# Band and cross probabilities in one tile, with 2 KB rows in the transfers inside SBUF

## The chip, the cores and the metric

The kernel runs on one core of a Trainium2 chip. The time is the device time of one execution in microseconds; below it is the median of three runs. A profile of one further execution gives the trace that the prediction reads. TensorE is PE (and PEld for its weight loads), VectorE is DVE, ScalarE is ACT, GpSimd is POOL, and SP is the engine that issues most of the DMA transfers.

## The reference

One layer of a decoder trunk is computed for a prompt of 4096 tokens and for 8 sequences of 8 new tokens ("sample"). The model width is 1024. What the kernel computes for the prompt, cut to the core:

```python
h = rmsnorm(x, g_pre);  z = h @ w_in                      # one combined projection
out_a = silu(cg) * cb * conv3(cc * ch)                    # 256 channels
o_b = window attention, 8 heads of 64 in 2 kv groups,     # 128-query blocks, keys of this
      window 128, one learned sink per head               # and the previous block
out_b = silu(ag) * o_b
o_c = cross attention, 4 heads of 64, into 256 memory tokens
out_c = silu(mg) * o_c
y = concat(out_a, out_b, out_c) @ w_out
result = x + rmsnorm(y, g_post)
```

For the sample the same layer runs with cached window keys and values, cached memory keys and values and a cached convolution state.

## The kernel before

The kernel has two stages. The first, up to about 970 us, is the input projection: TensorE multiplies split fp32 operands (a high and a low part) in a seven-product scheme. Near its end the first two groups of attention (`early_scores`, `early_transposes`, `early_values`) are put between its products.

The second stage runs over 33 blocks of 128 tokens (block 32, the sample, goes before block 31). `Block.run` multiplies the gated mix of one block with `w_out`: two halves of 512 columns, each of 8 x 3 matmuls (high by high, low by high, high by low) into one PSUM bank, `y_0` and `y_1`. Between these matmuls it runs the events of `events_of(i)`, keyed by the half and the step at which they come. Block i works on three attention groups at once:

- `values_and_scores(i)` at (0, 0): `Group.scores` multiplies queries and keys of group i + 3 (PSUM tiles `ws`, band, and `xs`, cross), then `Group.values` multiplies the finished probabilities of group i + 1 with the values (PSUM tile `pv`) and multiplies the result into the gates (`mix` or `place`); then the softmax of group i + 3 ends.
- `turn(0, i + 3)` and `turn(1, i + 3)` at (1, 2): `turn_band` and `turn_cross` transpose the probabilities on VectorE in 32 x 32 squares, and transfers inside SBUF move the squares to their partitions.
- `turn(2, i + 2)` at (0, 4): `masks` applies the window's two triangles on GpSimd to the moved band probabilities.
- `blocks[i + 1].split` at (1, 3): the next block's mix is split in a high part (ACT) and a low part (DVE) for TensorE.

Band probabilities of a group are in a tile `sm`, cross probabilities in a tile `xp`, each of 128 x 1024 fp32. Odd groups have a buffer of their own in the pool `wp`; even groups take theirs from the pool `work`, which has three buffers of 4 KB per partition. `moved` issues 16 transfers for one tile, 32 partitions by 1 KB each, so that a group takes 32 of them on SP:

```python
src = squares.rearrange("p (k n) -> p k n", k=4)
for g in range(4):
    for k in range(4):
        DMA.dma_start(to[32 * k : 32 * k + 32, g], src[32 * g : 32 * g + 32, k])
```

The end of a block is in two tails that run in the next block's `scores`: `scale` (the root mean square; the power is taken on GpSimd) and `store` (VectorE multiplies by that factor and adds the residual `xr`, line 1581; SP stores the result to `o_yp`). `xr` has two buffers, so that the load for block b + 2 on SP waits until the store of block b has landed. The other transfers on SP in this stage are `vh` (values of a group) and, for every second block, the gates of a chunk of 256 tokens (`mix` or `place`, 1 MB). Keys and queries of a chunk (`kst`, `q`) are loaded by GpSimd's queue.

Instructions are placed by a scheduler, except those that `keep_in_program_order` pins on their engine: in the blocks 1 to 30 all of VectorE's (`InOrder`), the masks, the high part of the split, and the attention's matmuls after the first (`tiled`). In the order that comes out, `y_0` of a block (18 or all 24 of its matmuls) stands between the scores and the values.

Of the kernel before, what the change touches and what calls it, by code (L numbers as in the profile page):

```python
# [8 lines left out]
F32 = mybir.dt.float32  # L9
# [3 lines left out]
ALU = mybir.AluOpType  # L13
AX = mybir.AxisListType

P = 128
D = 1024
KT = D // P
# [33 lines left out]
def hybrid_layer(ctx: ExitStack, tc: tile.TileContext, a: dict):  # L52
    nc = tc.nc
    TE, S, G, DMA = nc.tensor, nc.scalar, nc.gpsimd, nc.sync
# [981 lines left out]
    def work(name):  # L1036

        return third["work"].tile([P, D], F32, tag="u", name=name)

    run_open = [False]  # L1040

    def tiled(o, w, x, **kw):
# [69 lines left out]
    class Group:  # L1112
# [6 lines left out]
        def open_scores(self, n):  # L1119
            b = self.b  # L1120
            if n == 0:
                t = wp.tile([P, D], F32, tag="sm", name=f"sm{b}", bufs=1) if b % 2 and b > 1 else work(f"sm{b}")
                self.sm = t.rearrange("p (h k j) -> p h k j" if b < 2 else "p (k h j) -> p h k j", h=8, k=4)
                self.flat_sm = t
            if n == 3:
                t = wp.tile([P, D], F32, tag="p", name=f"xp{b}", bufs=1) if b % 2 and b > 1 else work(f"xp{b}")
                self.p = t.rearrange("p (h a k j) -> p h a k j" if b < 2 else "p (k h a j) -> p h a k j", h=4, a=2, k=4)
                self.flat_p = t

        def early_scores(self, n):  # L1130
            self.open_scores(n)
# [12 lines left out]
        def scores(self):  # L1144
            self.open_scores(0)
            self.open_scores(3)
# [50 lines left out]
        def band_weights(self):  # L1197
            n, (es, den, rd) = 8, self.band_sums
            V.tensor_tensor(den, den, es, op=ALU.add)
            V.reciprocal(rd, den)  # L1200
            V.tensor_scalar(rd, rd, 0.5, None, op0=ALU.mult)
            flat = self.flat_sm.rearrange("p (h k) -> p h k", h=n) if self.b < 2 else self.flat_sm.rearrange("p (k h j) -> p k h j", h=n, k=4)
# [19 lines left out]
        def early_transposes(self, n):  # L1222
            if n == 0:
                pt = work(f"wpt{self.b}").rearrange("p (u n) -> p u n", u=2)
                pv = work(f"wpv{self.b}").rearrange("p (u n) -> p u n", u=2) if self.b else None
                for u in range(2):
                    self.pt[u], self.pv[u] = pt[:, u], pv[:, u] if self.b else None
            if n == 2:
                xpt = work(f"xpt{self.b}").rearrange("p (u n) -> p u n", u=2)
                for u in range(2):  # L1230
                    self.xpt[u] = xpt[:, u]
            if n < 2:
                self.band_transposes(n, psum(0, f"wt{self.b}_{n}"))
            else:
                self.cross_transposes(n - 2, psum(0, f"xt{self.b}_{n}"))

        def moved(self, squares, name):

            tc.keep_in_program_order(V.transpose(squares, squares))
            to = wp.tile([P, 4, 256], F32, tag=name, name=f"{name}{self.b}")  # L1240
            src = squares.rearrange("p (k n) -> p k n", k=4)
            for g in range(4):
                for k in range(4):
                    DMA.dma_start(to[32 * k : 32 * k + 32, g], src[32 * g : 32 * g + 32, k])
            return to

        def turn_band(self):
            self.w = self.moved(self.flat_sm, "wt").rearrange("p g (h i) -> p g h i", h=8)

        def turn_cross(self):  # L1250
            self.x = self.moved(self.flat_p, "xt").rearrange("p g (h a i) -> p g h a i", h=4, a=2)

        def masks(self):

# [176 lines left out]
    def sample_window():  # L1431
# [22 lines left out]
        both = work("ssm")[:, : 4 * 192].rearrange("p (a n) -> p a n", a=4)  # L1454
# [30 lines left out]
        pt, ptn = work("swpt").rearrange("p (a n) -> p a n", a=2)[:, 0], work("swptn")[:64, :512]  # L1485
# [21 lines left out]
    class Block:  # L1507
# [28 lines left out]
        def run(self, last, events):  # L1536
# [6 lines left out]
            for p, (c0, c1) in enumerate(parts):  # L1543
                if b == 0:
                    both = values_psum("y0") if p == 0 else both
                    acc = both[:, p]
                else:
                    acc = (values_psum(f"y{b}_1")[:, 1] if p == 1 else psum(p // 2, f"y{b}_{p}"))[:, : c1 - c0]
                j, passes = 0, 3 if m == P else 2
                for k in range(KT):  # L1550
                    for fn in events.get((min(p, 1), k), ()) if p < 2 else ():
                        fn()
                    for l, r in ((0, 0), (1, 0), (0, 1)) if m == P else ((0, 0), (0, 1)):
                        TE.matmul(acc, self.hl[l][:, k], wo[k][c0 // 512][:, r, c0 % 512 : c0 % 512 + c1 - c0], start=j == 0, stop=j == passes * KT - 1)  # L1554
                        j += 1
                if m < P:
                    S.copy(yn[:m, c0:c1], acc[m : 2 * m])
                    V.tensor_tensor(acc[:m], acc[:m], yn[:m, c0:c1], op=ALU.add)
                end = last and p == 2
                if not end:  # L1560
                    V.tensor_tensor(yn[:m, c0:c1], acc[:m], gpost[:m, c0:c1], op=ALU.mult)
                square = lambda acc=acc, p=p, c0=c0, c1=c1, end=end: S.activation(  # L1562
                    (psum(2, "sq") if end else acc)[:m, : c1 - c0], acc[:m], AF.Square, scale=float(D) ** -0.5, accum_out=st[:m, p : p + 1])
                if p == 0 or last or b == 32:
                    square()
                if last and p == 1:
                    V.tensor_tensor(st[:m, 0:1], st[:m, 0:1], st[:m, 1:2], op=ALU.add)
# [9 lines left out]
                    V.tensor_tensor(yn[:m, 768:D], acc[:m], gpost[:m, 768:D], op=ALU.mult)  # L1577

            def store():
                for cs in (slice(0, 512), slice(512, D)) if last else (slice(0, D),):  # L1580
                    V.scalar_tensor_tensor(self.xr[:m, cs], yn[:m, cs], st[:m, 3:4], self.xr[:m, cs], op0=ALU.mult, op1=ALU.add)  # L1581
                    DMA.dma_start(dst[:, cs], self.xr[:m, cs])
# [23 lines left out]
    def events_of(i):  # L1606
# [3 lines left out]
        def at(p, k, fn, *args):  # L1610
            ev.setdefault((p, k), []).append(lambda: fn(*args))
# [141 lines left out]
```

## Time and profile before

| | |
|---|---|
| median of three runs | 1812.81 us (1812.52 to 1813.56) |
| the profiled execution | 1814.48 us, span 1812.8 us |
| mean granted clock of TensorE in it | 0.926 |
| PE busy | 1537.6 us (85%) |
| PEld busy | 1380.1 us (76%) |
| DVE busy | 1197.3 us (66%) |
| ACT busy | 732.0 us (40%) |
| POOL busy | 344.2 us (19%) |
| SP's DMA queue (q1) | 194501 packets, 262.47 MB, 46.9% of 16 engines |
| POOL's DMA queue (q0) | 40800 packets, 69.76 MB, 14.8% |

A row of the timeline has the start, the duration, the engine, the line of the kernel, the operation, what it writes and reads, and how many instructions are merged in the row; a bracket gives the idle time before it and what ended that. SPq is SP issuing transfers. A row of the waits has who waited for whom, the time in total, the number of waits and the longest. A row of the groups has the instructions of one line and form, their number, busy time, mean duration in ns, and the idle time before them.

### The profile page before, as it was taken

The numbers are of one execution on the slowest core, as the hardware profiler recorded it, in microseconds if no ns is written. First come the engines' busy times: TensorE is split into PE (matmuls) and PEld (weight loads), VectorE is DVE, ScalarE is ACT, GpSimd is POOL, SyncE is SP. The second block draws the span as 40 slices with busy tenths as digits, with TensorE's granted clock in tenths as the row PEclk, the third lists the DMA queues.
The fourth block names the chain that finished last, engine by engine and source line by source line (L and its number), as shares of the span: only waits on it lengthen the run. The fifth ranks groups of instructions, "written<-read, shape, count | busy, mean of one in ns | idle before, by whom it ended". The sixth has DMA issues, their size and how long they took to land. (4 is left out here: it accounts for less than half of the span.)

```text
span 1812.8 us, 31491 instructions
## 1 busy us (share of the span) xinstructions
PE 1537.6 (85%) x11471; PEld 1380.1 (76%) x11471; DVE 1197.3 (66%) x1920; ACT 732.0 (40%) x1844; POOL 344.2 (19%) x522
## 2 busy tenths in 40 slices
PE   9999999999999999999995776678667766777548
PEld 9999999999999999999994555456555555555336
DVE  7788888998877797677684654455546545654414
ACT  6766565642222244454362333333333333333212
POOL 0223332230000000001002322233123223322200
PEclk9999999999999999999997898888888888988679
DMA  9989998776432379677877455543554554343342
GB/s 259 215 230 268 269 237 297 245 211 233 165 107 107 121 258 306 222 238 231 247 286 204 131 158 156 154 113 121 150 156 133 155 156 138 111 136 116 121 157 82
DMA packets 236175, 335.29 MB, mean 185 GB/s; under 512 B 62453, under 2 KB 164853, under 8 KB 235989
## 3 DMA queue, kind: packets, MB, share of 16 engines
q1 hardware_dynamic: 194501, 262.47, 46.9%
q0 software_dynamic: 40800, 69.76, 14.8%
q8 instruction: 91, 1.49, 0.4%
q10 hardware_dynamic: 720, 1.05, 0.2%
q14 instruction: 63, 0.52, 0.1%
HBM read 192.54 MB, written 110.15 MB: 167 GB/s over the span
## 5 line engine op out<-in xcount | busy, mean ns | idle before, releaser
L1554 PE MATMUL y<-wo,mh 128*128 128x512 f32 (+1 forms) x1040 | 340.2, 400 | 41.3 <-DVE sm L62 13.1
L1554 PEld LDWEIGHTS y<-wo,mh 128*128 128x128 f32 x1040 | 198.4, 192 | 103.1 <-issue 33.5
L377 DVE TENSOR_TENSOR z<-c,z 128x520 f32<-128x520 f32 (+1 forms) x308 | 195.0, 646 | 88.8 <-PE c L370 88.0
L1554 PE MATMUL y<-wo,ml 128*128 128x512 f32 (+1 forms) x520 | 204.8, 394 | 0.0
L1044 PE MATMUL pv<-xt,mv 128*64 128x128 f32 x480 | 54.4, 398 | 176.6 <-DMA xt<-xp 108.8
L1044 PEld LDWEIGHTS pv<-xt,mv 128*64 128x64 f32 x480 | 43.9, 207 | 188.2 <-issue 181.8
L1212 ACT ACTIVATE xp<-xs,xnm 128x256 f32<-128x256 f32 x128 | 58.9, 473 | 260.8 <-issue 127.7
L1220 POOL TENSOR_SCALAR xp<-xp,xrd 128x256 f32<-128x256 f32 x128 | 62.4, 502 | 490.5 <-DVE xrd L62 404.0
L1195 ACT ACTIVATE sm<-sm,wnm 128x128 f32<-128x128 f32 x256 | 99.1, 389 | 116.9 <-DVE wnm L62 113.8
L62 DVE TENSOR_TENSOR mix<-mix,pv 128x256 f32<-128x256 f32 (+1 forms) x32 | 16.3, 551 | 159.0 <-PE pv L1044 153.8
L1554 PEld LDWEIGHTS y<-wo,ml 128*128 128x128 f32 x520 | 100.2, 193 | 20.5 <-issue 2.0
L62 DVE TENSOR_TENSOR place<-place,pv 128x256 f32<-128x256 f32 (+1 forms) x28 | 14.3, 551 | 134.3 <-PE pv L1044 134.3
L1178 ACT COPY sm<-ws 128x256 f32<-128x256 f32 x128 | 41.2, 376 | 68.1 <-PE ws L1044 43.2
L1562 ACT ACTIVATE y<-y 128x512 f32<-128x512 f32 (+1 forms) x66 | 38.4, 582 | 72.4 <-DVE yn L62 63.8
L1258 POOL TENSOR_SCALAR_AFFINE_SELECT wd<-wt 128x512 f32<-128x512 f32 (+1 forms) x60 | 60.8, 1013 | 32.0 <-DMA wt<-sm 16.5
L1044 PEld LDWEIGHTS ws<-kst,q 64*128 64x128 f32 x768 | 48.9, 190 | 11.6 <-issue 5.6
L62 DVE SCALAR_TENSOR_TENSOR xr<-yn,yst,xr 128x1024 f32<-128x1024 f32 x30 | 42.8, 1427 | 21.1 <-POOL yst L1575 21.0
L1044 PE MATMUL ws<-kst,q 64*128 64x256 f32 x768 | 56.5, 293 | 0.0
L1044 PE MATMUL pv<-wt,vh 128*64 128x256 f32 x240 | 53.0, 583 | 0.0
L745 POOL MEMSET negs<- 128x1 f32 x1 | 0.1, 98 | 264.4 <-PE c L370 264.4
L283 ACT ACTIVATE nat<-nat 104x1024 f32<-104x1024 f32 x40 | 42.2, 1056 | 15.7 <-DMA nat<-in_x_p 15.7
L1195 ACT ACTIVATION_READ_ACCUMULATOR sm<-sm,wnm 128x1 f32 x256 | 48.1, 188 | 0.0
(979 smaller groups left out, 4971.0 us busy)
## 6 DMA issues: line engine op xcount, KB each, us to landing
q<-qd POOLq DMA_DIRECT2D x32, 768.0 KB, 9.1
xr<-in_x_p SPq DMA_DIRECT2D x32, 512.0 KB
nat<-in_x_p SPq DMA_DIRECT2D x39, 416.0 KB
o_yp<-xr SPq DMA_DIRECT2D x31, 512.0 KB
wt<-sm SPq DMA_DIRECT2D x480, 32.0 KB
xt<-xp SPq DMA_DIRECT2D x480, 32.0 KB
md<-th POOLq DMA_DIRECT2D x48, 260.0 KB, 7.4
qd<-zh SPq DMA_DIRECT2D x48, 260.0 KB
```

Of the source, the lines that this page charges most:

```text
L62: return (lambda *args, **kw: tc.keep_in_program_order(fn(*args, **kw))) if self.on else fn
L283: S.activation(t[:RG], t[:RG], AF.Square, accum_out=r[:RG, i : i + 1])
L377: add = lambda dst, other: V.tensor_tensor(dst, c, other, op=ALU.add)
L745: G.memset(third["negs"], NEG)
L1044: ins = TE.matmul(o, w, x, **kw)
L1178: S.copy(to, squares(s3[:, :, P : 2 * P]))
L1195: S.activation(sm[:, h], sm[:, h], AF.Exp, bias=nm[:, h : h + 1], scale=SCALE, accum_out=den[:, h : h + 1])
L1212: S.activation(p[:, i], s[:, i].rearrange("p (a k j) -> p a k j", a=2, k=4), AF.Exp, bias=nm[:, i : i + 1], scale=SCALE, accum_out=den[:, ...
L1220: G.tensor_scalar(p[:, i], p[:, i], rd[:, i : i + 1], 0.5, op0=ALU.mult, op1=ALU.mult)
L1258: G.affine_select(out, src, pattern=[[32 * sign, 2], [0, 8], [sign, 32]], compare_op=op, fill=0.0, base=base * sign, channel_multiplier=-s ...
L1554: TE.matmul(acc, self.hl[l][:, k], wo[k][c0 // 512][:, r, c0 % 512 : c0 % 512 + c1 - c0], start=j == 0, stop=j == passes * KT - 1)
L1562: square = lambda acc=acc, p=p, c0=c0, c1=c1, end=end: S.activation((psum(2, "sq") if end else acc)[:m, : c1 - c0], acc[:m], AF.Square, sc ...
```

## The change

- One tile of 128 x 2048 holds band and cross probabilities. For group 2 and after, each of the four 32-column squares has 256 band columns and 256 cross columns side by side, so that one transfer moves 32 partitions by 2 KB: 16 transfers a group instead of 32. Even groups take the tile from `work` (now one buffer of each size), odd ones from `wp`. The two transposes stay separate; all transfers are issued after the second.
- The masks of group i + 2 move from event (0, 4) to (1, 1).
- The residual: ScalarE multiplies by the factor, and GpSimd adds `xr`, both pinned; VectorE's instruction goes, except for the last two blocks.
- The first matmul of each half-block, and the first after each event, are pinned. In the order that comes out, the values come right after the scores in every block, and all of `y_0` and `y_1` after them.
- The first groups and the sample's window reuse parts of the larger tile; the load of the sample's mask (`smraw`) comes earlier on SP.

```diff
-        third["work"] = right.enter_context(tc.tile_pool(name="work", bufs=3, side="right"))
+        third["work"] = right.enter_context(tc.tile_pool(name="work", bufs=1, side="right"))
...
+    def pair(name):
+
+        return third["work"].tile([P, 2 * D], F32, tag="uu", name=name)
...
+        def open_scores(self):
             b = self.b
+            t = wp.tile([P, 2 * D], F32, tag="s", name=f"s{b}", bufs=1) if b % 2 and b > 1 else pair(f"s{b}")
+            if b < 2:
+                self.flat_sm, self.flat_p = t[:, :D], t[:, D:]
...
+            else:
+                self.squares = t.rearrange("p (k n) -> p k n", k=4)
+                self.sm = self.squares[:, :, :256].rearrange("p k (h j) -> p h k j", h=8)
+                self.p = self.squares[:, :, 256:].rearrange("p k (h a j) -> p h a k j", h=4, a=2)
...
-        def moved(self, squares, name):
-
-            tc.keep_in_program_order(V.transpose(squares, squares))
-            to = wp.tile([P, 4, 256], F32, tag=name, name=f"{name}{self.b}")
-            src = squares.rearrange("p (k n) -> p k n", k=4)
+        def turn_band(self):
+            part = self.squares[:, :, :256]
+            tc.keep_in_program_order(V.transpose(part, part))
+
+        def turn_cross(self):
+            part = self.squares[:, :, 256:]
+            tc.keep_in_program_order(V.transpose(part, part))
+            to = wp.tile([P, 4, 512], F32, tag="w", name=f"w{self.b}")
             for g in range(4):
                 for k in range(4):
-                    DMA.dma_start(to[32 * k : 32 * k + 32, g], src[32 * g : 32 * g + 32, k])
-            return to
+                    DMA.dma_start(to[32 * k : 32 * k + 32, g], self.squares[32 * g : 32 * g + 32, k])
...
+                    ordered = b > 0 and (j == 0 or p < 2 and (min(p, 1), k) in events)
                     for l, r in ((0, 0), (1, 0), (0, 1)) if m == P else ((0, 0), (0, 1)):
-                        TE.matmul(acc, self.hl[l][:, k], ...)
+                        ins = TE.matmul(acc, self.hl[l][:, k], ...)
+                        if ordered:
+                            tc.keep_in_program_order(ins)
+                        ordered = False
...
             def store():
+                if not last and b != 32:
+                    tc.keep_in_program_order(S.mul(yn, yn, st[:, 3:4]))
+                    G.tensor_tensor(self.xr, yn, self.xr, op=ALU.add)
+                    DMA.dma_start(dst, self.xr)
+                    return
...
-        at(0, 4, turn, 2, i + 2)
+        at(1, 1, turn, 2, i + 2)
```

More of the change, by code (lines that the diff above doesn't have):

```diff
@@ L1038, in work, with in_order_here @@
         return third["work"].tile([P, D], F32, tag="u", name=name)
+    def pair(name):
+        return third["work"].tile([P, 2 * D], F32, tag="uu", name=name)
+    def in_order_here(ins):
+        if ps is not None:
+            tc.keep_in_program_order(ins)
     run_open = [False]
@@ L1117, in __init__, with early_scores @@
             self.pt, self.pv, self.xpt, self.cross_sums = {}, {}, {}, {}
-        def open_scores(self, n):
+        def open_scores(self):
             b = self.b
-            if n == 0:
[L1122 to L1131, printed above, removed]
+            t = wp.tile([P, 2 * D], F32, tag="s", name=f"s{b}", bufs=1) if b % 2 and b > 1 else pair(f"s{b}")
+            if b < 2:
+                self.flat_sm, self.flat_p = t[:, :D], t[:, D:]
+                self.sm = self.flat_sm.rearrange("p (h k j) -> p h k j", h=8, k=4)
+                self.p = self.flat_p.rearrange("p (h a k j) -> p h a k j", h=4, a=2, k=4)
+            else:
+                self.squares = t.rearrange("p (k n) -> p k n", k=4)
+                self.sm = self.squares[:, :, :256].rearrange("p k (h j) -> p h k j", h=8)
+                self.p = self.squares[:, :, 256:].rearrange("p k (h a j) -> p h a k j", h=4, a=2)
+        def early_scores(self, n):
+            if n == 0:
+                self.open_scores()
             if n < 2:
@@ L1144, in scores @@
         def scores(self):
-            self.open_scores(0)
-            self.open_scores(3)
+            self.open_scores()
             bands = [psum(n, f"ws{self.b}_{n}").rearrange("p (h k) -> p h k", h=2) for n in range(4)]
@@ L1201, in band_weights @@
             V.tensor_scalar(rd, rd, 0.5, None, op0=ALU.mult)
-            flat = self.flat_sm.rearrange("p (h k) -> p h k", h=n) if self.b < 2 else self.flat_sm.rearrange("p (k h j) -> p k h j", h=n, k=4)
+            flat = self.flat_sm.rearrange("p (h k) -> p h k", h=n) if self.b < 2 else self.squares[:, :, :256].rearrange("p k (h j) -> p k h j", h=n)
             rd = rd.unsqueeze(2).to_broadcast([P, n, P]) if self.b < 2 else rd.unsqueeze(1).unsqueeze(3).to_broadcast([P, 4, n, 32])
@@ L1224, in early_transposes @@
                 pt = work(f"wpt{self.b}").rearrange("p (u n) -> p u n", u=2)
-                pv = work(f"wpv{self.b}").rearrange("p (u n) -> p u n", u=2) if self.b else None
+                pv = self.flat_sm.rearrange("p (u n) -> p u n", u=2) if self.b else None
                 for u in range(2):
@@ L1235, in early_transposes @@
                 self.cross_transposes(n - 2, psum(0, f"xt{self.b}_{n}"))
-        def moved(self, squares, name):
-            tc.keep_in_program_order(V.transpose(squares, squares))
-            to = wp.tile([P, 4, 256], F32, tag=name, name=f"{name}{self.b}")
-            src = squares.rearrange("p (k n) -> p k n", k=4)
+        def turn_band(self):
[5 more added lines that the diff above has]
+            to = wp.tile([P, 4, 512], F32, tag="w", name=f"w{self.b}")
             for g in range(4):
                 for k in range(4):
-                    DMA.dma_start(to[32 * k : 32 * k + 32, g], src[32 * g : 32 * g + 32, k])
-            return to
[L1247 to L1251, printed above, removed]
+                    DMA.dma_start(to[32 * k : 32 * k + 32, g], self.squares[32 * g : 32 * g + 32, k])
+            self.w = to[:, :, :256].rearrange("p g (h i) -> p g h i", h=8)
+            self.x = to[:, :, 256:].rearrange("p g (h a i) -> p g h a i", h=4, a=2)
         def masks(self):
@@ L1453, in sample_window @@
         transpose_to(svn, [(zs[:, 5, :], 64)], 1, "svnt")
-        both = work("ssm")[:, : 4 * 192].rearrange("p (a n) -> p a n", a=4)
+        ssm = pair("ssm")
+        both = ssm[:, : 4 * 192].rearrange("p (a n) -> p a n", a=4)
         sms = [both[:, 2 * half : 2 * half + 2] for half in range(2)]
@@ L1484, in sample_window @@
         yield
-        pt, ptn = work("swpt").rearrange("p (a n) -> p a n", a=2)[:, 0], work("swptn")[:64, :512]
+        pt, ptn = ssm[:, D : D + 512], ssm[:64, D + 512 : 2 * D]
         transpose_to(pt, [(sm[i][:, 0:P], P) for i in range(4)], 1, "swt0")
@@ L1552, in run @@
                         fn()
+                    ordered = b > 0 and (j == 0 or p < 2 and (min(p, 1), k) in events)
                     for l, r in ((0, 0), (1, 0), (0, 1)) if m == P else ((0, 0), (0, 1)):
-                        TE.matmul(acc, self.hl[l][:, k], wo[k][c0 // 512][:, r, c0 % 512 : c0 % 512 + c1 - c0], start=j == 0, stop=j == passes * KT - 1)
+                        ins = TE.matmul(acc, self.hl[l][:, k], wo[k][c0 // 512][:, r, c0 % 512 : c0 % 512 + c1 - c0], start=j == 0, stop=j == passes * KT - 1)
+                        if ordered:
+                            tc.keep_in_program_order(ins)
+                        ordered = False
                         j += 1
```

## The prediction

> **What bounds the kernel now.** I read the page's slices first, then busy time by stretches, then SP's queue in order of time.
>
> ```profile
> PE   9999999999999999999995776678667766777548
> ```
> ```profile
> 600.00:700.00 100.00, 98.46 (x818) 98.08 (x818) 84.83 (x125) 38.08 (x54) 2.36 (x4) 1.00 0.62 208
> 1200.00:1400.00 200.00, 145.65 (x905) 110.19 (x902) 110.17 (x206) 66.38 (x255) 54.95 (x83) 0.84 0.51 143
> ```
>
> Columns: stretch, length, busy PE, PEld, DVE, ACT, POOL (instructions), granted TensorE clock, DMA share, GB/s. The input projection keeps TensorE at 98% of the time at full clock. From about 970 us, in attention, it is busy 73% at clock 0.84, and no engine is full: DVE 55%, ACT 33%, POOL 27%. Something outside the engines sets the pace. SP's queue over two blocks:
>
> ```profile
> 1352.95 0.53 SPq L1582 DMA_DIRECT2D o_yp<-xr  x1
> 1353.57 0.38 SPq L1110 DMA_DIRECT2D vh<-vn  x1
> 1354.13 1.93 SPq L1244 DMA_DIRECT2D wt<-sm  x3
> 1356.16 0.54 SPq L1516 DMA_DIRECT2D xr<-in_x_p  x1
> 1356.74 9.00 SPq L1244 DMA_DIRECT2D wt<-sm  x13
> 1365.84 10.06 SPq L1244 DMA_DIRECT2D xt<-xp  x16
> 1376.00 0.54 SPq L1582 DMA_DIRECT2D o_yp<-xr  x1
> 1376.64 0.49 SPq L1090 DMA_DIRECT2D mix<-md  x1
> 1383.03 0.34 SPq L1516 DMA_DIRECT2D xr<-in_x_p  x1
> 1383.46 0.38 SPq L1110 DMA_DIRECT2D vh<-vn  x1
> 1384.02 11.11 SPq L1244 DMA_DIRECT2D wt<-sm  x16
> 1395.23 10.26 SPq L1244 DMA_DIRECT2D xt<-xp  x16
> 1405.60 0.52 SPq L1582 DMA_DIRECT2D o_yp<-xr  x1
> ```
> ```profile
> SPq L1516 <- DMA o_yp<-xr: 64.2, 12, 6.4
> 1364.10 1.24 DVE L62 STREAM_TRANSPOSE sm<-sm 128x1024 f32<-128x1024 f32 x1
> 1365.51 1.25 DVE L62 STREAM_TRANSPOSE xp<-xp 128x1024 f32<-128x1024 f32 x1 [0.17 <-POOL xp L1220]
> PE pv L1044 <- DMA xt<-xp: 89.6, 16, 9.0
> ```
>
> Two blocks take 1405.60 - 1352.95 = 52.65 us, 26.3 each. SP issues in 45.6 us of it and stands 5.9 us (1377.13 to 1383.03) at the load of xr, which waits for the store of the buffer that it reuses (12 such waits between 1050 and 1650 us: every other block). SP has no slack. The group whose transposes end at 1366.76 gets its first transfer at 1384.02, 17 us later. TensorE's largest wait, for xt, is that queue.
>
> **The change: half the transfers.** Each block's 32 transfers of 32 x 1 KB become 16 of 32 x 2 KB. One costs 10.06/16 = 0.63 us of SP now.
>
> ```profile
> 1395.00:1402.00 7.00, 6.93 (x44) 5.41 (x42) 5.98 (x11) 2.88 (x12) 4.22 (x5) 1.00 0.18 47
> ```
>
> What does a 2 KB row cost? In this stretch only these transfers run, and the DMA engines are busy 18%: 0.18 x 0.63 = 0.11 us of each engine per transfer. Twice that, 0.23, still fits in 0.63. The store of 512 KB takes 0.53 us to issue, so issue doesn't follow bytes. Bounds: 0.53 (nearest large transfer from SBUF) and 1.26 (everything follows bytes). I take 0.63, since rows and queue are the same kind, and SP saves 16 x 0.63 = 10 us a block. [...]
>
> SP per pair of blocks becomes 2 x 10.1 (transfers), 1.1 (o_yp), 0.8 (vh), 0.5 (mix), 0.9 (xr), 1.3 gaps, and the waits for o_yp: 5.9 in the block with mix, up to 1.5 in the other. That is 31 to 32, or 15.4 to 16.1 a block.
>
> **What is late next: TensorE.**
>
> ```profile
> 1043.65 1.09 PE L1044 MATMUL pv<-xt,mv 128*64 128x128 f32 x16 [2.27 <-DMA xt<-xp]
> 1046.13 0.50 PE L1554 MATMUL y<-wo,ml 128*128 128x512 f32 x1
> 1381.52 1.98 PE L1044 MATMUL pv<-xt,mv 128*64 128x128 f32 x16 [7.36 <-DMA o_yp<-xr]
> 1386.19 0.80 PE L1554 MATMUL y<-wo,mh 128*128 128x512 f32 x1
> 1388.00 0.63 PE L1554 MATMUL y<-wo,mh 128*128 128x512 f32 x2
> 1392.77 0.62 PE L1554 MATMUL y<-wo,mh 128*128 128x512 f32 x2
> 1393.77 1.70 PE L1044 MATMUL ws<-kst,q 64*128 64x256 f32 x24
> 1396.16 0.51 PE L1554 MATMUL y<-wo,mh 128*128 128x512 f32 x1
> 1005.88 1.70 PE L1044 MATMUL ws<-kst,q 64*128 64x256 f32 x24
> 1650.09 1.69 PE L1044 MATMUL ws<-kst,q 64*128 64x256 f32 x24
> ```
>
> After 2.27 us of idling the values (pv) take 2.48 us; after 7.36 they take 4.67, as the clock has dropped. So without long waits a block is pv 2.5, scores 2.4 (1393.77 to 1396.16), and 48 y matmuls at 0.227 (21 between 1388.00 and 1392.77): 10.9. Sum 15.8, against 25.8 now (1005.88, scores in block 2, to 1650.09 in block 27: 25 blocks, 644.2 us).
>
> **The rest of the edit, on this 15.8 us clock.**
>
> ```profile
> 1400.59 0.40 ACT L1195 ACTIVATE sm<-sm,wnm 128x128 f32<-128x128 f32 x1 [3.52 <-DVE wnm L62]
> L1212 ACT ACTIVATE xp<-xs,xnm 128x256 f32<-128x256 f32 x93 | 42.8, 472 | 218.1 <-issue 98.2 <-DMA wt<-sm 61.9 <-DVE xnm L62 20.7
> L1220 POOL TENSOR_SCALAR xp<-xp,xrd 128x256 f32<-128x256 f32 x96 | 44.1, 475 | 373.5 <-DVE xrd L62 355.6 <-DMA wt<-sm 17.9
> ```
>
> The new order of instructions puts pv right behind the scores, where 18 or 24 y matmuls stood between; y's first matmul after each event is pinned. That costs nothing if w has landed. When it lands: the band exponentials start 6.8 us after the scores (1393.77 to 1400.59), 5.3 without DVE's xr step; then 8 x 0.4, 4 cross exponentials at 0.47, 4 weights at 0.475, small steps 0.5 and a transpose of 1.25 make 14.0. SP issues until 24, 2 to 3 us to land (the xr load at 1356.16 didn't wait for the store of 1352.95), masks 3.3: 30. pv is due at 2 x 15.8 + 2.4 = 34. So 4 us of cover, and beyond it each us is paid. That the band half now waits for the cross half costs the 1.4 us between the two transposes, inside this sum.
>
> ```profile
> L1258 POOL TENSOR_SCALAR_AFFINE_SELECT wt<-wt 128x512 f32<-128x512 f32 x46 | 32.1, 720 | 1.5
> L476 POOL TENSOR_TENSOR cacc<-cacc,z 128x64 f32<-128x64 f32 x4 | 1.6, 393 | 0.3
> L1530 ACT CAST mh<-mix 128x1024 fp32r<-128x1024 f32 x12 | 12.5, 1039 | 0.0
> L62 DVE SCALAR_TENSOR_TENSOR xr<-yn,yst,xr 128x1024 f32<-128x1024 f32 x23 | 33.5, 1455 | 19.6 <-POOL yst L1575 19.6
> ```
>
> DVE loses 1.46 us a block: 110.17 per 200 us is 14.4 a block, so 13.0 stay. ACT gains about 1.04 (8.7 to 9.7) between its score copies and the band exponentials; these wait for DVE's maximum until 5.3 us anyway, and the multiply, behind the square, the power step and its own 1.04, ends near 4.5, so it is covered; without that cover it costs up to 1.04 a block. If the power step on POOL is late, ACT's exponentials queue behind the multiply, and DVE's weights behind them. POOL gains an add of 1024 columns: at least 2 x 0.72 = 1.4, at most 16 x 0.39 = 6.3 (by 64-column pieces); I take 2.5, nearer the first since size, not start-up, rules it. POOL stays under 7.2 + 6.3 = 13.5, so neither end moves the sum. [...] Queued behind the add are o_yp on SP, then xr, then the next w. Masks move from the first to the second half of the block and now always stand before the power step on POOL: the wait for w holds that step, its multiply and the exponentials, free while w lands within the cover. Pools (work 3 to 1 buffer, one pair tile) hold the same bytes; a score tile is reused two groups later, after its transfers: nothing, with 6 us to spare (26 against 32.6). The smask load moves ahead: in the tail.
>
> **The sum**, against the execution of 1814.48 us (span 1812.8; 1.67 above the median of 1812.81, so a forecast span serves as a forecast median).
>
> ```profile
> 964.71 16.48 SPq L1244 DMA_DIRECT2D wt<-sm  x16
> PE sms L1398 <- DMA sq<-in_cmk: 33.1, 4, 14.1
> ```
>
> Head, to the scores of block 2: 1006 now. The first group's 16 transfers took 16.48 us among other loads and 10 more of xt followed; the 10 go, the start moves about 3 us back behind the cross transposes, and the first half of y of block 1 (24 x 0.227 = 5.5) no longer fills the wait: -2 (from -7 to +2): 1004. Middle, 25 blocks: TensorE's 15.8 and SP's 15.4 to 16.1 nearly coincide and alternate, so I take 1 us a block of friction: 16.8, 420 us. Tail, 1650.09 to the end: 162.7 now; four blocks save 9 each, and of the 33.1 us at the sample loads, queued behind a halved stream, half goes: 162.7 - 36 - 16 = 111 (94 to 138). Total 1004 + 420 + 111 = **1535**.
>
> **Rivals.** *A, a new wait at xr* (chance 0.17). If the store takes 5.9 us to land in every block, SP's block is 16 x 0.63 to 0.69 + 0.5 + 0.5 + 5.9 + 0.4 + 0.4 + gaps, about 19: 1004 + 475 + (162.7 - 27 - 16) = 1599. For it: order on the queue is unchanged, and traffic per us rises by half. Against: POOL's loads of keys and queries, beside mix now, go out a block apart from it.
> *Bytes rule* (0.03): a 2 KB transfer takes near 1.26 us, SP keeps 20 us a block, and the time stays at 1813. Against: share 0.18.
> *Slower* (0.05): the transfer costs more than 32 x 0.63 / 16 = 1.26 us, because larger rows also slow each other among the loads (11.11 for 16 where other loads ran). From there each 0.1 us adds 1.6 a block; at 1.35, 1.5 x 29 blocks = +43: 1856. Against: the same.
> *Forecast* (0.73): SP no longer the bound, 15.8 to 18 a block. The last 0.02: between A and no change.
>
> **Range.** Low: 1002 + 25 x 15.8 + 97 = 1495. High: rival A at 20 a block with a tail of 136: 1640. The measurement tells 0.2%, about 4 us, from no change. Faster: 0.73 + 0.17 + 0.02 = 0.92; same 0.03; slower 0.05.
>
> **What would show it.** Right: SP's 16 transfers in about 10 us a block with idle time ahead of them, pv 2.5 us after the scores without a wait over 2 us, clock 1.00 between 1100 and 1350, ws-to-ws near 16.8. Rival A: a wait for o_yp before each xr and pv waiting for w. Wrong: a pitch near 1.26 us a transfer; POOL's add over 6 us; or exponentials waiting for POOL's power step.

## The result, and the profile after

The changed kernel takes 1521.96 us (1520.57 to 1522.59, four runs) against 1812.69 us of the kernel before beside it: a ratio of 0.8394, 95% interval 0.838 to 0.8409. The forecast was 1535 us.

The slices of the page and one stretch of the middle, as shown of before:

```profile
PE   9999999999999999999999999599999999999787
PEclk9999999999999999999999999799999999999989
1200.00:1400.00 200.00, 199.74 (x1427) 158.16 (x1426) 178.88 (x317) 122.53 (x448) 119.10 (x156) 1.00 0.91 228
```

TensorE was busy 73% of such a stretch, at clock 0.84. Now it is busy all of it (199.74 of 200 us), at clock 1.00. The dip in slice 26 is the start of attention, the 787 at the end is the tail. VectorE is at 89%, and the DMA engines went from 0.51 to 0.91.

SP's queue over three blocks, then SP's and TensorE's waits between 1050 and 1350 us (who waits for whom, total, times, longest):

```profile
1157.53 0.53 SPq L1595 DMA_DIRECT2D o_yp<-xr  x1
1158.16 0.41 SPq L1098 DMA_DIRECT2D mix<-md  x1
1160.92 0.34 SPq L1524 DMA_DIRECT2D xr<-in_x_p  x1
1161.37 12.54 SPq L1256 DMA_DIRECT2D w<-s  x16
1174.00 0.53 SPq L1595 DMA_DIRECT2D o_yp<-xr  x1
1174.63 1.33 SPq L1118 DMA_DIRECT2D vh<-vn  x2
1177.12 0.51 SPq L1256 DMA_DIRECT2D w<-s  x1
1179.35 0.33 SPq L1524 DMA_DIRECT2D xr<-in_x_p  x1
1179.72 10.29 SPq L1256 DMA_DIRECT2D w<-s  x15
1193.94 11.26 SPq L1256 DMA_DIRECT2D w<-s  x16
```
```profile
SPq L1524 <- DMA o_yp<-xr: 32.7, 18, 3.0
SPq L1256 <- DMA w<-s: 13.8, 15, 2.1
SPq L1256 <- DVE s L62: 11.9, 9, 2.5
PEld pv L1052 <- POOL w L1265: 3.6, 9, 0.5
```

Sixteen transfers of 2 KB rows take 10.8 to 12.5 us here, 0.68 to 0.78 us each on average. The longest row, cut in two, shows what the average hides:

```profile
1161.37 9.90 SPq L1256 DMA_DIRECT2D w<-s  x15
1173.39 0.51 SPq L1256 DMA_DIRECT2D w<-s  x1
```

Fifteen transfers follow each other 0.66 us apart, then SP stands 2.1 us, by the profile for earlier transfers, before the last. Between 1050 and 1350 us the median distance of two such transfers is 0.63 us, as it was before; 32 of 275 stand more than 0.7 us apart, at most 2.7. So the larger rows did not make a transfer dearer to issue; what was added are single stops. SP now also waits for VectorE's transposes (11.9 us in 9 waits), and all of that still fits into a block. TensorE's wait for the transfers (89.6 us in 16 waits between 1050 and 1650 us of before) is gone; 0.4 us every other block is left, for the masks.

```profile
1001.21 1.69 PE L1052 MATMUL ws<-kst,q 64*128 64x256 f32 x24
1161.36 1.69 PE L1052 MATMUL ws<-kst,q 64*128 64x256 f32 x24
1163.70 1.09 PE L1052 MATMUL pv<-w,mv 128*64 128x128 f32 x16
1165.59 0.66 PE L1052 MATMUL pv<-wd,vh 64*64 64x256 f32 x8
1401.98 1.69 PE L1052 MATMUL ws<-kst,q 64*128 64x256 f32 x24
```

The scores of block 2 start at 1001.21, those of block 27 at 1401.98: 25 blocks at 16.03 us. These two marks cut a run into head, middle and tail. The same marks in every profiled run:

| profiled run | span | head | one block | tail |
|---|---|---|---|---|
| before | 1812.8 | 1005.9 | 25.77 | 162.7 |
| changed kernel | 1520.6 | 1001.2 | 16.03 | 118.6 |
| changed kernel, second and third | 1527.7, 1530.4 | 1008.1, 1010.9 | 16.04, 16.05 | 118.6, 118.1 |
| 32 transfers, halved by columns | 1801.6 | 1015.2 | 25.22 | 156.0 |
| 32 transfers, halved by rows | 1837.0 | 1016.1 | 26.62 | 155.4 |
| 32 transfers, two queues | 1739.0 | 1018.6 | 23.62 | 129.9 |
| 16 transfers, half the bytes | 1575.2 | 1011.8 | 18.31 | 105.6 |
| merged tile alone, twice | 1516.2, 1523.2 | 1005.9, 1010.9 | 15.97, 15.99 | 110.9, 112.7 |
| residual back on VectorE | 1532.7 | 1014.3 | 15.99 | 118.6 |
| old order, residual moved | 1526.1 | 1010.7 | 16.05 | 114.1 |
| merged tile, both ends changed | 1528.4 | 1010.2 | 15.98 | 118.8 |
| merged tile, loads ahead | 1509.5 | 1005.7 | 15.99 | 104.2 |

The chips differ a little (before: 1812.7 to 1821.7 us), and the head varies: from 1001.2 to 1010.9 us between the three runs of the changed kernel, to 1018.6 over all of the table. Most of that is there before attention begins: the first scores start at 782.3 us in the kernel before, at 783.7 in the changed kernel's first run, and at 787.1 to 795.0 in all others. From there to the scores of block 2 it is 223.6 us before and 217.3 to 218.1 in the changed kernel's three runs. Even the ratio to the kernel before on the same chip came out at 0.8394, 0.8433 and 0.8399 for the changed kernel. So differences of half a per cent are read from blocks and tails, not from whole times.

### The profile page after: what moved, and what is told of

Read it like the earlier page. It is cut to its first block, busy times and chain, and to the rows that moved or that the text cites. A ratio compares the mean times of both kernels' runs of the same rounds, so it can differ in the third digit from the quotient of the medians.

```text
span 1520.6 us, 30844 instructions
## 1 busy us (share of the span) xinstructions
PE 1474.7 (97%) x11471; PEld 1344.8 (88%) x11471; DVE 1206.0 (79%) x1889; ACT 761.0 (50%) x1875; POOL 414.8 (27%) x553
## 5 line engine op out<-in xcount | busy, mean ns | idle before, releaser
L1204 ACT ACTIVATE s<-s,wnm 128x128 f32<-128x128 f32 x256 | 99.1, 389 | 43.9 <-DVE wnm L62 40.8
L1229 POOL TENSOR_SCALAR s<-s,xrd 128x256 f32<-128x256 f32 x128 | 62.6, 504 | 169.1 <-DVE xrd L62 106.5
L1187 ACT COPY s<-ws 128x256 f32<-128x256 f32 x128 | 41.2, 378 | 113.4 <-PE ws L1052 85.9
L1594 POOL TENSOR_TENSOR xr<-yn,xr 128x1024 f32<-128x1024 f32 x31 | 74.5, 2402 | 22.8 <-ACT yn L1593 22.5
L62 DVE STREAM_TRANSPOSE s<-s 128x1024 f32<-128x1024 f32 x56 | 68.5, 1237 | 2.9 <-POOL s L1229 2.9
L1265 POOL TENSOR_SCALAR_AFFINE_SELECT wd<-w 128x512 f32<-128x512 f32 (+1 forms) x60 | 54.9, 915 | 52.8 <-DMA w<-s 28.1
L62 DVE TENSOR_TENSOR yn<-y,gpost 128x512 f32<-128x512 f32 x60 | 41.0, 683 | 29.6 <-PE y L1563 28.3
L1221 ACT ACTIVATE s<-xs,xnm 128x256 f32<-128x256 f32 x128 | 58.3, 464 | 4.1 <-DVE xnm L1219 3.2
L62 DVE COPY_PREDICATED s<-wmask,ws 128x256 f32<-128x256 uint8 x112 | 43.5, 442 | 16.4 <-ACT s L1187 12.5
L1265 POOL TENSOR_SCALAR_AFFINE_SELECT w<-w 128x512 f32<-128x512 f32 x60 | 48.1, 824 | 2.1
L1593 ACT ACTIVATE yn<-yn,yst 128x1024 f32<-128x1024 f32 x31 | 35.6, 1149 | 25.6 <-POOL yst L1587 25.6
```

What stands on the lines that cost most here:

```text
L62: return (lambda *args, **kw: tc.keep_in_program_order(fn(*args, **kw))) if self.on else fn
L1187: S.copy(to, squares(s3[:, :, P : 2 * P]))
L1204: S.activation(sm[:, h], sm[:, h], AF.Exp, bias=nm[:, h : h + 1], scale=SCALE, accum_out=den[:, h : h + 1])
L1221: S.activation(p[:, i], s[:, i].rearrange("p (a k j) -> p a k j", a=2, k=4), AF.Exp, bias=nm[:, i : i + 1], scale=SCALE, accum_out=den[:, ...
L1229: G.tensor_scalar(p[:, i], p[:, i], rd[:, i : i + 1], 0.5, op0=ALU.mult, op1=ALU.mult)
L1265: G.affine_select(out, src, pattern=[[32 * sign, 2], [0, 8], [sign, 32]], compare_op=op, fill=0.0, base=base * sign, channel_multiplier=-s ...
```

## The experiments

The theory: SP's issuing was the bound, at a price per transfer and not per byte; halving the transfers left TensorE as the bound; the residual and the order gave nothing. Rivals: the order or the moved residual made the gain; bytes, or rows, set the price of a transfer.

**Twice the transfers, the same bytes.** Two kernels take back the count alone. The first halves each transfer by columns:

```diff
-                    DMA.dma_start(to[32 * k : 32 * k + 32, g], self.squares[32 * g : 32 * g + 32, k])
+                    for cs in (slice(0, 256), slice(256, 512)):
+                        DMA.dma_start(to[32 * k : 32 * k + 32, g, cs], self.squares[32 * g : 32 * g + 32, k, cs])
```

> The changed kernel with every transfer of the pair tile split in two again (32 transfers of 32 rows x 1 KB a block, the band half and the cross half), all else as in the changed kernel. Theory (SP's issuing was the bound, about 0.63 us for each transfer whatever its rows hold): SP gets 32 x 0.63 = 20.2 us, 1.3 us of other transfers and 2 to 4 us of stops, 24 to 26 us a block, and the time goes back to 1001 + 25 x 25 + 117 = 1743 us (1715 to 1790). Rival 1 (the gain came from the new order and the moved residual): those are kept, so about 1522 us. Rival 2 (the moved bytes set the time): the bytes are the same, so about 1522 us.

Measured: 1799.94 us, 0.988 of before (0.985 to 0.991). The order and the moved residual are still in, and nearly all of the gain is gone. This doubles the rows too (32 of 1 KB each), so the second halves by rows, 16 rows of 2 KB:

```diff
+                    for r in (0, 16):
+                        DMA.dma_start(to[32 * k + r : 32 * k + r + 16, g], self.squares[32 * g + r : 32 * g + r + 16, k])
```

> The changed kernel with each transfer cut by rows, not by columns: 32 transfers of 16 rows x 2 KB a block; bytes and rows of a block stay as in the changed kernel, only the count of transfers doubles. Theory (SP pays by the transfer): pitch 0.60 to 0.72 us, SP 22 to 27 us a block, time 1720 to 1810 us. Rival (it pays by the row that a transfer holds, so that 32 rows cost 0.63 us and 16 rows half): pitch 0.35 us, SP 13 us a block, time within 1% of the changed kernel.

Measured: 1837.27 us, 1.0102 of before (1.0065 to 1.014). SP's queue, by columns (two rows) and by rows (two rows):

```profile
1149.45 17.91 SPq L1257 DMA_DIRECT2D w<-s  x28
1171.71 23.08 SPq L1257 DMA_DIRECT2D w<-s  x32
```
```profile
1160.83 19.24 SPq L1257 DMA_DIRECT2D w<-s  x30
1189.65 22.32 SPq L1257 DMA_DIRECT2D w<-s  x32
```

The pitch (the time from one transfer to the next) is 0.64 to 0.72 us by these rows, and its median is 0.63 us whether a transfer is 32 rows of 1 KB, 16 rows of 2 KB or 32 rows of 2 KB. Rows and bytes did not set the pitch here; the time went with the count. The DMA engines behind the queue were not full: between 1050 and 1369 us their share was 0.54 by columns and 0.52 by rows, against 0.93 in the changed kernel, which moves the same bytes in shorter blocks. The blocks, 25.2 and 26.6 us, came as forecast (24 to 26, 22 to 27 for SP). Both times lie above their ranges, a miss, mainly because the tail, taken at 117 us, went back to 155 too.

**Half the bytes in the same 16 transfers.**

```diff
-                    DMA.dma_start(to[32 * k : 32 * k + 32, g], self.squares[32 * g : 32 * g + 32, k])
+                    DMA.dma_start(to[32 * k : 32 * k + 32, g, 0:256], self.squares[32 * g : 32 * g + 32, k, 0:256])
...
-            self.x = to[:, :, 256:].rearrange("p g (h a i) -> p g h a i", h=4, a=2)
+            self.x = to[:, :, :256].rearrange("p g (h a i) -> p g h a i", h=4, a=2)
```

> The changed kernel with its 16 transfers a block cut to the band half: 16 x 32 rows x 1 KB, half the bytes; the cross values then read the band weights in place of the cross ones. Theory (TensorE is the bound now, SP pays by the transfer): the steady blocks stay at 16.0 us, the time at 1515 to 1523 us, and SP's pitch stays at 0.60 to 0.66 us a transfer; what it falls below the 0.63 to 0.78 us of the changed kernel is the part that comes from full DMA engines. Rival (a transfer costs by its bytes): the pitch falls to about 0.35 us. If the steady blocks become shorter than 15.9 us, TensorE was not the bound.

This kernel leaves out the transfer of the cross probabilities, so it doesn't compute the layer. Measured: 1573.64 us, 0.8635 of before (0.8603 to 0.8667), slower than with all bytes, which neither theory expected. The queue, and the chain of a slow block:

```profile
1155.44 10.91 SPq L1256 DMA_DIRECT2D w<-s  x16
1193.16 10.03 SPq L1256 DMA_DIRECT2D w<-s  x16
1171.89 1.51 POOL L1265 TENSOR_SCALAR_AFFINE_SELECT wd<-w 128x512 f32<-128x512 f32 x2 [7.26 <-DMA o_yp<-xr]
1176.73 1.25 DVE L62 STREAM_TRANSPOSE s<-s 128x1024 f32<-128x1024 f32 x1 [5.76 <-POOL s L1229]
1180.56 1.98 PE L1052 MATMUL pv<-w,mv 128*64 128x128 f32 x16 [5.55 <-issue]
```

The pitch is 0.63 to 0.68 us at half the bytes, and its median 0.63 again, so the rival of a price by bytes (0.35 us) falls. Stops are rarer: 10 of 247 distances are above 0.7 us, against 32 of 275. On its time the run says little, since the scheduler's order came out different as well. In the slow blocks the masks stand ahead of the cross weights on GpSimd and wait 7.26 us, by the profile for a transfer; the weights queue behind them, and VectorE's transpose waits 5.76 us for these. Behind it on VectorE comes the product that ScalarE's square of y waits for; that square ends at 1180.46, and TensorE, idle for 5.55 us, starts pv at 1180.56 (its row names no releaser). The changed kernel has the masks behind the weights (L1229 at 1173.96, masks from 1178.19). Why the masks waited that long is open.

**The transfers on two queues.** Of the 32 of 1 KB rows, those with `g == 3` go out on ScalarE's queue:

```diff
+                        (S if g == 3 else DMA).dma_start(to[32 * k : 32 * k + 32, g, cs], self.squares[32 * g : 32 * g + 32, k, cs])
```

> As the run with 32 transfers of 1 KB rows, but 8 of the 32 are issued on ScalarE's queue and 24 on SP's. Theory (each queue issues its transfers one after another, and that is what bounds): SP falls to 24 x 0.65 + 1.3 + 2 = 18.9 us a block, ScalarE rises to 8.9 + 8 x 0.65 = 14 us; time 1001 + 25 x 19 + 117 = 1593 us (1550 to 1640). Rival (the number of transfers or packets loads the DMA engines behind all queues): the time stays within 2% of that with all 32 on SP.

Measured: 1739.99 us, 0.9551 of before (0.953 to 0.9572): 3.3% below the run on one queue and 147 us above the forecast, a miss. SP's queue (one row), then ScalarE, TensorE and a transpose on VectorE:

```profile
1183.37 18.02 SPq L1257 DMA_DIRECT2D w<-s  x24
1182.49 6.99 ACTq L1257 DMA_DIRECT2D w<-s  x8
1189.53 1.04 ACT L1539 CAST mh<-place 128x1024 fp32r<-128x1024 f32 x1 [7.56 <-DMA w<-s]
1193.20 1.98 PE L1052 MATMUL pv<-w,mv 128*64 128x128 f32 x16 [5.05 <-ACT y L1575]
1184.86 1.25 DVE L62 STREAM_TRANSPOSE s<-s 128x1024 f32<-128x1024 f32 x1 [2.53 <-POOL s L1229]
```

SP's 24 cost 18.0 us here, 15.6 in the forecast, and ScalarE's 8 cost 6.99 us. The two queues did not slow each other's pace: between 1050 and 1350 us, while ScalarE issues too, the median distance is 0.65 us on SP and 0.64 on ScalarE. What was added are stops: SP's waits ahead of these transfers come to 17.3 us for VectorE's transposes (17 times) and 15.9 us for earlier transfers (17 times, at most 3.7 us), and ScalarE's 8 take longer than at its pace, too. Here each queue stands until VectorE's second transpose, that of the cross half, ends at 1186.11, which the profile names as what released both; the other stops are not worked out. And ScalarE stands 7 us at its 8, with the split, the score copies and the square of y queued behind them, and TensorE waits 5.05 us for that square before pv. The relief of one queue became a wait on another engine. So the whole time decides little; that the price belongs to the queue, and not to the engines behind it, is read from the pitch and from the shares above.

**The merged tile alone.** The kernel before with one tile and 16 transfers; residual, order and masks as before:

> The kernel before with the merged tile and its 16 transfers alone: the residual's scale and add back on VectorE in one instruction, the masks back at their old place early in the block, no pinned y matmuls. Theory (halving SP's transfers is the whole mechanism): SP 13 us, VectorE 14.4 us, TensorE 15.8 us a block, so TensorE still bounds, with up to 1 us of friction from the values waiting for the masks: 1545 us (1522 to 1580), 80% or more of the gain of 291 us. Rival (the residual's move or the order is needed as well): over 1620 us.

Measured: 1518.76 us, 0.8348 of before (0.832 to 0.8376), a little below the forecast's range. Not 80% of the gain but all of it: 15.97 us a block, TensorE full (318.78 of the 319 us from 1050). Then beside the changed kernel on one chip:

> The changed kernel once more, on one chip with the merged tile alone, since the two have not yet been timed on the same chip. Expected steady blocks of 16.03 us, a tail of 118.6 us from the last steady block's scores to the end.

> The merged tile with its 16 transfers alone, once more, beside the changed kernel. Theory (the residual's move and the pinned order gave nothing in the steady blocks and 7.7 us less in the tail without them): steady blocks 15.97 us against 16.03, tail 110.9 us against 118.6, head within 5 us either way: 5 to 9 us less than the changed kernel (0.3% to 0.6%). Rival (the difference of the first comparison was that of two chips): within 0.1%.

The medians are 1526.17 us (0.8399, 0.8374 to 0.8425) for the changed kernel and 1523.22 us (0.8375, 0.8353 to 0.8398) for the merged tile alone. They are 3 us apart, 5 to 9 were forecast, and the intervals overlap: whole times don't tell the two apart. The traces show a tail 5.4 to 7.7 us shorter and blocks 0.06 us shorter for the merged tile alone.

**Residual and order, one at a time**, with the changed kernel as yardstick:

```diff
-                if not last and b != 32:
-                    tc.keep_in_program_order(S.mul(yn, yn, st[:, 3:4]))
-                    G.tensor_tensor(self.xr, yn, self.xr, op=ALU.add)
-                    DMA.dma_start(dst, self.xr)
-                    return
```

> The changed kernel itself, beside the three others of this set on one chip: the yardstick for differences under one per cent. Expected 0.8394 of the kernel before (0.838 to 0.841) and steady blocks of 16.03 us.

> The changed kernel with the residual's scale and add back on VectorE in one instruction; order and masks as changed. Theory 1 (TensorE bounds the steady blocks, and the add on GpSimd cost VectorE as much as it saved): steady blocks 16.0 us, VectorE 13.7 us a block (it gets 1.28 us for the residual and loses about 1.8 us of stretching: wnm 167 ns in place of 1375, xnm 169 in place of 397), time within 0.3% of the changed kernel. Rival (the residual's move was worth something, as the prediction had it for VectorE: 1.46 us a block): VectorE 15.5 us and the time up by 5 us or more.

Measured: 1529.68 us for the yardstick (0.8433, 0.8408 to 0.8457), above the 0.838 to 0.841 expected, though its blocks are 16.04 us; and 1526.15 us with the residual on VectorE (0.8412, 0.8386 to 0.8437). Groups of VectorE between 1050 and 1369 us, 20 blocks, changed kernel (its first run) first, then residual back:

```profile
L62 DVE SCALAR_TENSOR_TENSOR wnm<-wmx,nsink 128x8 f32<-128x8 f32 x20 | 27.5, 1375 | 0.7
L62 DVE TENSOR_SCALAR xnm<-xmx 128x2 f32<-128x2 f32 x40 | 15.9, 397 | 1.4
1050.00:1369.00 319.00, 318.72 (x2309) 251.91 (x2306) 283.32 (x498) 192.62 (x700) 188.37 (x230) 1.00 0.93 230
```
```profile
L62 DVE SCALAR_TENSOR_TENSOR xr<-yn,yst,xr 128x1024 f32<-128x1024 f32 x20 | 25.6, 1278 | 3.0 <-POOL yst L1587 2.9
L62 DVE TENSOR_SCALAR xnm<-xmx 128x2 f32<-128x2 f32 x40 | 6.8, 169 | 1.4
L62 DVE SCALAR_TENSOR_TENSOR wnm<-wmx,nsink 128x8 f32<-128x8 f32 x20 | 3.3, 167 | 0.7
1050.00:1369.00 319.00, 318.76 (x2310) 253.17 (x2308) 272.01 (x519) 170.08 (x680) 135.83 (x210) 1.00 0.89 230
```

With the residual's 25.6 us back, VectorE is busy 11 us less (272.0 against 283.3): wnm and xnm alone fall by 33.3 us. Moving the residual took nothing off VectorE. TensorE bounds both, and the two intervals of the time overlap.

The old order, with the residual moved (`ordered = False`, masks back at (0, 4)):

> The changed kernel with the old order: no pinned y matmuls, masks back at their old place; the residual stays moved (ScalarE and GpSimd). Theory (order touches only the two ends): steady blocks 16.0 us; the head up by 4 to 5 us (values of the first groups later) and the tail down by 7 to 8 us (y matmuls fill the wait for the sample loads), so 3 us less than the changed kernel (0 to 6). Rival (the pinned order is what lets TensorE run without gaps): steady blocks of 16.5 us or more, over 10 us more time.

Measured: 1522.1 us (0.8389, 0.8367 to 0.8412); blocks 16.05 us, tail 114.1. The rival falls: unpinned, TensorE has no gaps either. The tail gains 4.5 us, less than the 7 to 8 forecast, and the head did not move measurably (218.0 us from the first scores to those of block 2, where 4 to 5 us more were forecast). The time is 7.6 us below the yardstick, outside the forecast of 0 to 6, but the intervals overlap. What the tail gains is seen in the block where the sample's first scores wait for their keys; the changed kernel, then the merged tile alone:

```profile
1410.44 0.62 PE L1405 MATMUL sms<-sq 128*32 128x256 f32 x2
1418.83 1.95 PE L1405 MATMUL sms<-sq 128*32 128x256 f32 x14 [7.77 <-DMA sq<-in_cmk]
```
```profile
1413.74 0.62 PE L1405 MATMUL sms<-sq 128*32 128x256 f32 x2
1424.27 1.95 PE L1405 MATMUL sms<-sq 128*32 128x256 f32 x14 [2.65 <-DMA sq<-in_cmk]
```

Pinned y matmuls stay behind the waiting ones; unpinned ones fill most of that gap. TensorE's idle time there is 7.7 to 9.3 us in the four runs with the pins and 2.1 to 2.9 us in the three without them.

**The ends.** With TensorE full in the middle, only head and tail are left. The wait for the keys comes from SP's order: in the changed kernel their second half is issued at 1411.48 us, behind 16 transfers from 1400.78. Two kernels on the merged tile alone:

```diff
         for j in range(2):
             DMA.dma_start(km[:, j], a["cmk"][j][:, bs])
+        yield
+        for j in range(2):
             DMA.dma_start(vm[:, j], a["cmv"][j][:, bs])
...
-    sample = {(26, 1, 4): mem0,
+    sample = {(26, 0, 3): mem0, (28, 0, 3): mem1, (26, 1, 4): mem0,
...
+                    (S if self.b < 3 and g % 2 else DMA).dma_start(to[32 * k : 32 * k + 32, g], self.squares[32 * g : 32 * g + 32, k])
```

> The kernel with the merged tile alone, and two changes at its ends: the sample's key loads are issued before the 16 transfers of that block, not behind them, and 8 of the first group's 16 transfers go on ScalarE's queue. Theory (TensorE is full in the steady blocks, so only the ends can still give anything): steady blocks 15.97 us; tail 2 to 6 us shorter, head 0 to 6 us shorter, so 3 to 11 us less than with the merged tile alone, a ratio of 0.829 to 0.834 to the kernel before. Rival (the ends wait for something else, such as the loads' own length): no difference from the merged tile alone, 0.835.

Measured: 1529.37 us (0.8426, 0.8407 to 0.8445), above the forecast of 0.829 to 0.834. The merged tile alone was not run on this chip, so the traces decide: no gain, a tail of 118.8 us in place of 110.9 to 112.7. The first wait went (the scores of blocks 27 and 28 stand 20.6 us apart, not 25.2), and two others came, one for the window keys and one in the window's transposes (SP's queue, TensorE, and a row of TensorE's waits in the tail):

```profile
1461.40 0.38 SPq L1444 DMA_DIRECT2D skc<-in_cwk  x1
1468.36 0.69 PE L1473 MATMUL sws<-skc 128*64 128x128 f32 x4 [5.89 <-DMA skc<-in_cwk]
PE swt L1379 <- DVE ssm L62: 5.0, 1, 5.0
```

The window keys (skc), issued at 1420.43 with the merged tile alone, had now fallen behind another block's 16 transfers, and TensorE stood 5.89 us for them. The head lost 3.5 us (blocks 1 to 2: 29.4 us against 25.9) with ScalarE issuing, where a gain of 0 to 6 was forecast. The second kernel leaves the head alone and puts skc ahead as well, at (27, 0, 4):

> The merged tile alone, with the sample's loads (memory keys, window keys) issued ahead of the 16 transfers of their blocks, not behind them. Theory: the wait at the first sample scores goes (the two scores of its block stand 20.6 us apart in place of 25.2), the window scores no longer wait for their keys, and the tail falls from 110.9 to 103 to 107 us, the time 4 to 8 us below the merged tile alone. Rival (another wait takes their place, as in the run with both ends changed): no gain.

Measured: 1511.16 us, 0.8313 of before (0.8287 to 0.8338), 12 us below the merged tile alone beside it, more than the 4 to 8 forecast. Of that the tail, 104.2 us, gives 6.8 to 8.5 us, as expected. The rest lies before attention, where no gain was meant: in the two profiled runs on that chip the first scores start at 787.1 and 793.3 us, within the spread seen above.

```profile
1413.82 1.09 PE L1407 MATMUL sms<-sq 128*32 128x256 f32 x16
1448.14 0.44 PE L1474 MATMUL sws<-skc 128*64 128x128 f32 x4
```

Neither waits any more. By its ratio and its tail it is the fastest version measured.

## Why the prediction was right, point by point

- **SP bound, and pays by the transfer: right.** Doubling the count alone brings nearly all of the old time back (1799.94 and 1837.27 us). The pitch was taken at 0.63 us, and that is its median; with its stops a block's transfers average 0.68 to 0.78. SP and TensorE were forecast nearly level, and that had no price: SP now stands idle for VectorE's transposes (the 11.9 us above), which is slack.
- **TensorE next, at 15.8 us: right**, 16.03 measured. The 1 us of friction was a mis-sized term: 0.2 us. SP and TensorE nearly coincide, but don't alternate as bounds. That is 19 us of the sum (420 forecast, 400.8 measured).
- **Head 1004:** 1001.2 in that run, but 1008.1 and 1010.9 in two others, so the agreement is partly luck. From the first scores to block 2 the change gave 5.5 to 6.3 us, where the sum booked 2 (from -7 to +2).
- **Tail 111 (94 to 138):** 118.6. Its two terms erred in opposite directions. "Half of the wait at the sample loads goes" was too careful: 33.1 us became 7.8 (the row below), which is 25 gone where 16 were booked. "Four blocks save 9 each" was the mis-sized term: all the rest of the tail gave 19 us of the 36. The 9 comes from steady blocks, and the tail was not made of such blocks: TensorE stood 59 us of it before, and 33 of these at the sample loads, in the same blocks. The sum also had no cost for the pins: without them the tail is 114.1 us, and 110.9 to 112.7 with the merged tile alone.

```profile
PE sms L1405 <- DMA sq<-in_cmk: 7.8, 1, 7.8
```

- **4 us of cover for pv:** there is next to none. The scores at 1145.27 belong to the transfers from 1161.37 to 1173.90; forecast 14 to 24 us after the scores, they came 16.1 to 28.6 us after. The masks run from 1178.19 to 1181.18, and pv starts at 1179.64; its part without masks goes first. The 0.4 us waits for POOL above are this edge. The price stayed small by the order of pv's parts, not by the cover, and that was luck.
- **Stop at xr:** rival A's wait is there, in nearly every block, but at 1.8 us on average, 3.0 at most, not 5.9. SP had room for it.
- **POOL's add 2.5 us:** 2.41 (below). **ACT's multiply 1.04:** 1.15, covered: it ends 4.3 us after the scores, where 4.5 was forecast (1165.68 in the block of 1161.36).
- **VectorE down to 13.0 us: wrong.** 283.32 / 319 x 16.03 = 14.2, and 13.6 with the residual on VectorE. (By the mean block of 25.8 us the start, too, was 14.2 and not 14.4: nothing was saved.) The step took the removed instruction as the whole of it and looked for what stretches beside the new one only on the engines that received work.
- **Clock 1.00 and pv at 2.5 us:** right, 2.55 us (1163.70 to 1166.25) at clock 1.00. In the kernel before, the granted clock was 1.00 in the pv after 2.27 us of idling and 0.50 in the one after 7.36 us (the column behind POOL's):

```profile
1043.65:1046.13 2.48, 2.48 (x32) 1.62 (x33) 0.00 (x0) 0.00 (x0) 0.00 (x0) 1.00 0.61 193
1381.52:1386.19 4.67, 4.67 (x32) 2.84 (x32) 0.00 (x0) 0.00 (x0) 0.00 (x0) 0.50 1.01 356
```

The sum came within 1% because errors of -19, +8 and -3 us partly cancelled; the mechanism did not depend on that.

## What to carry to other kernels

Where one queue issues all day, count its instructions before its bytes: 16 transfers in place of 32 made a block 10 us shorter, while the same bytes in 32 cost nearly the whole gain. Once another engine is full, work moved between the engines behind it bought nothing here, and made one of them busier, so change one thing and read the block. Loads that a later stage needs belong ahead of a burst of transfers on the same queue (behind 16 of them, the sample's keys cost TensorE 7.77 us), and moving one load can push the next behind the next burst (5.89 us for the window keys).

## What the runs showed of the hardware that was not expected

In the changed kernel, some small VectorE instructions that run beside GpSimd's add last until the add ends. VectorE, then GpSimd:

```profile
1198.14 2.58 DVE L62 SCALAR_TENSOR_TENSOR wnm<-wmx,nsink 128x8 f32<-128x8 f32 x1
1216.26 1.18 DVE L62 TENSOR_SCALAR xnm<-xmx 128x2 f32<-128x2 f32 x1
```
```profile
1198.28 2.41 POOL L1594 TENSOR_TENSOR xr<-yn,xr 128x1024 f32<-128x1024 f32 x1
1215.02 2.40 POOL L1594 TENSOR_TENSOR xr<-yn,xr 128x1024 f32<-128x1024 f32 x1 [1.26 <-ACT yn L1593]
```

wnm, eight columns wide, ends at 1200.72 with the add's 1200.69; xnm, two columns, at 1217.44 with 1217.42. The same stands in all 20 blocks between 1050 and 1369 us: one instruction beside each add (wnm, xnm, once wes) ends 0.02 to 0.04 us after it. Out of the add's way, and in the run with the residual back on VectorE, these take 0.17 us. Others beside the same add are untouched: the reduction xmx takes 0.68 us there as in the run with the residual back, and the product of the gates with pv, 512 columns, 0.68 us in both. The time went by what was left of GpSimd's add, at eight columns as at two: wnm, begun 0.14 us before the add, took 2.58 us; xnm, begun 1.24 us into it, 1.18. That is 1.7 us a block (33.3 us over 20), more than the 1.28 us that the move took away. Why these last until the add ends was not tried.

The other surprise is how near the DMA engines may be to being next: by their share, 0.93 of a 16.03 us block is 14.9 us, where before it was 0.51 of 25.8, or 13.2 us. Their work per block grew by an eighth; the block shrank onto it. Whether they would bound next was not tried.
